# One more pair in seven products, and a new order of the last pairs, in the second run of two down projections

## The chip, the cores and the metric

The kernel runs on one core of a Trainium2 chip. The metric is the device time of one execution in microseconds (us); lower is better. A time of a kernel is the median over several runs. The profile shows one execution more, with every instruction of every engine: PE (TensorE, the matmuls), PEld (its weight loads), DVE (VectorE), ACT (ScalarE), POOL (GpSimd) and SP (SyncE, which here only issues transfers).

## The reference, cut to what matters

The kernel computes one encoder layer on 256 tokens of width 2048: a SwiGLU block, a mixer (gated recurrence and window attention), and a second SwiGLU block, each between RMS norms. The change touches the last matrix product of both SwiGLU blocks, `(silu(gate) * up) @ w_down`:

```python
def swiglu(x, w_gate_up, w_down):
    gate, up = jnp.split(x @ w_gate_up, 2, axis=-1)
    return (jax.nn.silu(gate) * up) @ w_down
...
    for layer in range(DEPTH):
        ff = swiglu(rms_norm(x, pre_norm_ffn1[layer]), w_ffn1_gate_up[layer], w_ffn1_down[layer])
        x = x + 0.5 * rms_norm(ff, post_norm_ffn1[layer])
        ...
        ff = swiglu(rms_norm(x, pre_norm_ffn2[layer]), w_ffn2_gate_up[layer], w_ffn2_down[layer])
        x = x + 0.5 * rms_norm(ff, post_norm_ffn2[layer])
```

`w_down` has 5632 rows and 2048 columns, in float32; the left side is 256 x 5632.

## The kernel before, in words

**Precision.** A float32 product is made of three matmuls in a faster format. Each operand is split into a high part `h` (a rounding copy on ACT, L177) and a low part `l` (source minus high part, on DVE, L178). Then high x high, high x low and low x high are added up in PSUM (`three`, L458 is its matmul).

**Pairs.** The 5632 inner rows are cut into 22 *pairs* of 2 x 128 rows, numbered 0 to 21. The 2048 output columns are cut into two *runs* of 1024. One run takes all 22 pairs and adds them up in four PSUM banks, `c[m][n]` (m: which 128 tokens, n: which 512 columns). So a pair in a run is a 2 x 2 by 2 x 2 block product, and it is done in one of two ways:

- *plain* (`play`, `plain`): eight block products, 24 matmuls of 128 x 128 by 128 x 512;
- *seven* (`products`): Strassen's scheme in Winograd's form, seven block products, 21 matmuls, some of them into four more banks `p`. It needs sums of blocks on both sides. The sums of the left side (`sums[u]`) are made once per pair, on DVE, either when the pair's activations are made (pairs 0 to 14, even) or later by `sums_again` (L1107 to L1114: one instruction of 128 x 512 and four of 128 x 128). Before use they are split in `left_sums` (tile `sp`); for pairs 0 and 2 the split sums of the first run are kept. The sums of the right side come from the weights: two are made by a transfer that adds into the tile (POOL, L1314), two by DVE (L1342, L1343).

At the end of a run a *fold* (`fold`, L548 to L565) combines the `p` banks and adds them into the `c` banks.

**Steps.** The two runs are one list of 44 *steps*, 0 to 43: `orders[0]` and then `orders[1]`; steps 22 to 43 are the second run. All of it is written in order by hand (`manual_schedule`), so each of PE, ACT and DVE works through its instructions as they stand in the code. In step i the loop at L1401 issues:

1. the first part of `splits(i+1)`, the splitting of the next step's weights. For a plain pair that is half 0. For a seven pair it is half 1 (`h`, `l`), the split of the left sums (`sp`), and L1342 and L1343, which need the adding transfer to be done;
2. `prepare(i+4)`, if that step is a seven pair in `added`: its first block is split into the tiles `ha` and `la`, and POOL issues the adding transfer (half a megabyte), behind `la`;
3. transfers that bring back some activations that were put away in DRAM (`fetch`: in the second run pairs 0, 5, 3 and 1, in steps 25, 26, 28 and 29);
4. the second part of `splits(i+1)`: the other half of a plain pair, or the upper sums of a seven pair;
5. the matmuls of step i;
6. for a seven pair, the last part of `splits(i+1)`;
7. `sums_again`, in the steps named in `again_at`.

`ha` and `la` have three buffers each (`rows.firsts = 3`), `h` and `l` five each.

**Weights.** Each step's weights come as one load of a megabyte on SP's queue (L1298) into a tile `raw`. There are five such tiles: three *lasting* ones and two that lie in the pool of the fetched activations (`back`) and may not take the weights of steps 41, 42 and 43 (`coming[0] < NU + 19` in L1294). A load is issued when the splitting of an earlier step has freed a tile (`load_down` at the end of `splits`). The list of loads, `in_order`, is the list of steps with those in `added` moved ahead by 3.5 places. As there are five tiles, a load takes the tile of the step whose splitting ended at that moment, five loads earlier in the list as long as no tile is passed over.

**End of the run.** Pairs 20 and 21 (steps 42 and 43) are *held*: their weights are split in step 40 and after step 41, and their 48 matmuls come bank by bank after the fold has reached each bank (`finish`). Step 41 is the last ordinary one; there the products are sorted by bank, so that the fold can begin. The input `X` of the residual addition (two transfers of a megabyte, L1555) is loaded into the room of the left sums of pairs 0 to 14, after the last of them has been read.

Lines that the prediction names: L177 and L178 (splits), L458 (matmuls), L1107 to L1114 (left sums made later), L1298 (loads), L1314 (adding transfers), L1342 and L1343 (right sums), L1555 (`X`).

Of the kernel before, what the change touches and what calls it, by code (L numbers as in the profile page):

```python
# [37 lines left out]
def hymba_layer_kernel(  # L38
# [37 lines left out]
    def nm(s):  # L76
        uid[0] += 1
        return f"{s}_{uid[0]}"
# [120 lines left out]
    def close_far():  # L199
        far["cm"].__exit__(None, None, None)  # L200
# [719 lines left out]
    def post_pool():  # L920
        return tc.tile_pool(name=nm("post"), bufs=4, reuse_waits="tile")
# [17 lines left out]
    MIXED = range(0, 20, 2)  # L939
# [142 lines left out]
    def ffn(gated, w_dn, post_gain, again, gain=None, lead=None, aside=None):  # L1082

        with ExitStack() as st:
# [6 lines left out]
            hts, sums, away = [], {}, {}  # L1091
# [98 lines left out]
            def some(steps, n):  # L1190
                for _ in range(n):
                    next(steps)
# [21 lines left out]
            def boundary(g, ahead):  # L1214

                a, b = room_for("z"), room_for("s")
                c, (p1, p5, p6, p7) = gated.c, gated.p
                add = nc.vector.tensor_tensor
                rest_of = gated.take(g, last)

                def bank(m, n):
                    for k in range(2):
                        rest_of[4 * k + 2 * m + n]()

                nc.scalar.copy(a, p1)
                add(c[0][0], c[0][0], a, ALU.add)
                add(b, p6, a, ALU.add)
                add(a, p7, b, ALU.add)
                add(c[1][0], c[1][0], a, ALU.add)  # L1229
                bank(0, 0)  # L1230
                bank(1, 0)
                add(b, p5, b, ALU.subtract)
                add(c[0][1], c[0][1], b, ALU.add)
                bank(0, 1)
                add(b, p5, a, ALU.subtract)
                add(c[1][1], c[1][1], b, ALU.add)  # L1236
                bank(1, 1)
                some(ahead, 2)

            def first_pairs(g, waiting):  # L1240

                gated.group(g)
                some(waiting, 1)
                gated.prepare(g, MIXED_IN[1])
                some(waiting, 1)
                ahead = gated.splits(g, 1)
                some(ahead, 2)
                gated.prepare(g, MIXED_IN[2])
                for one in gated.take(g, 0):
                    one()  # L1250
                some(waiting, 1)
                ahead = gated.splits(g, 2)
                some(ahead, 2)
                some(waiting, 1)
                some(ahead, 1)
                for one in gated.take(g, 1):
                    one()

            def pair_ahead(g, u):

                ahead = gated.splits(g, u + 1)
                next(ahead)
                if u + 1 == MIXED_IN[1]:
                    gated.prepare(g, MIXED_IN[3])
                next(ahead)
                for one in gated.take(g, u):
                    one()
                for _ in ahead:
                    pass
                if g == 1 and u == 5:  # L1270
                    sums_in(MIXED_IN[3])
                if u == 5 and 1 < g <= AWAY // 2 + 1:
                    put_away(2 * g - 4)
                    put_away(2 * g - 3)
# [1 line left out]
            orders = [  # L1276
                [9, 11, 8, 13, 10, 15, 12, 1, 0, 3, 14, 5, 16, 17, 2, 7, 4, 19, 6, 18, 20, 21],

                [2, 7, 4, 9, 6, 8, 11, 10, 13, 12, 17, 15, 0, 5, 14, 3, 16, 1, 18, 19, 20, 21],
            ]  # L1280
            added = {0: (12, 0, 14, 16, 2, 4, 6, 18), 1: (*MIXED, 17)}
            steps = [(r, u) for r in range(2) for u in orders[r]]
            in_order = sorted(
                (i - 3.5 if u in added[r] else i, i) for i, (r, u) in enumerate(steps)
# [35 lines left out]
            def splits(i):  # L1320
                if i >= 2 * NU - Pairs.HELD:
                    return
                r, u = steps[i]
                raw = raws[i]
                parts = got[i] = []
                b11, b12, b21, b22 = blocks(raw)
                if not as_seven(r, u):
                    parts.append(split_half(raw, 0))
                    yield
                    parts.append(split_half(raw, 1))  # L1330
                    load_down(raw)
                    yield
                    return
                four = raw.rearrange("p (i c) -> p i c", i=4)
                if i not in firsts:
                    first_block(i)
                    nc.vector.tensor_tensor(
                        four[:, 0:2], four[:, 0::3], four[:, 1:2].to_broadcast([P, 2, 512]), ALU.add
                    )
                parts.append(split_half(raw, 1))  # L1340
                rows.left_sums_ahead(u)
                nc.vector.tensor_tensor(b22, b11, b22, ALU.add)  # L1342
                nc.vector.tensor_tensor(b21, b22, b21, ALU.add)  # L1343
                yield
                parts.append(split_half(raw, 0))
                yield
                parts.append(split_half(raw, 1))
                load_down(raw)
                yield
# [13 lines left out]
            with tc.manual_schedule():  # L1363
                gated.prepare(1, MIXED_IN[0])
                some(gated.splits(1, 0), 2)
                for g in range(1, NG):
                    first_pairs(g, waiting)
                    for u in range(2, last - 1):
                        pair_ahead(g, u)
                    some(gated.splits(g, last), 2)  # L1370
                    if g < NG - 1:
                        gated.prepare(g + 1, MIXED_IN[0])
                    for one in gated.take(g, last - 1):
                        one()
                    boundary(g, gated.splits(g + 1, 0) if g < NG - 1 else splits(0))
                    waiting = units(gated.c, rest)
                    some(waiting, 2)
                room_cm.__exit__(None, None, None)
                close_far()
                back_cm = tc.tile_pool(name=nm("hb"), bufs=AWAY // 2, reuse_waits="tile")  # L1380
                back = back_cm.__enter__()
                fetch_at = {2: (1,), 3: (0,), 5: (3,), 6: (5,), 9: (2,), 10: (7,), 11: (4,), 13: (6,)}
                fetch_at.update({25: (0,), 26: (5,), 28: (3,), 29: (1,)})
                again_at = {8: 16, 14: 18, 24: 17}
                for u in MIXED[8:]:
                    sums[u] = None
                rows = Pairs(w_dn, orders, hts, sums, work, post_gain, near=MIXED[:2])
                rows.firsts = 3
                some(waiting, 2)
                ahead = splits(1)  # L1390
                some(ahead, 2)
                products(0)
                for _ in range(2):
                    load_down(back.tile([P, 2048], F32, tag="raw", name=nm("raw"), bufs=2))
                some(waiting, 1)
                ahead = splits(2)
                some(ahead, 2)
                some(waiting, 1)
                some(ahead, 1)
                products(1)  # L1400
                for i in range(2, 2 * NU - Pairs.HELD):  # L1401
                    if i == NU + 18:
                        back_cm.__exit__(None, None, None)
                        early_cm.__exit__(None, None, None)
                        post = rows.post = st.enter_context(post_pool())
                    ahead = splits(i + 1)
                    next(ahead, None)
                    prepare(i + 4)
                    for u in fetch_at.get(i, ()):
                        fetch(u)  # L1410
                    next(ahead, None)
                    if i == NU + 18:
                        rows.hold(1, raws[2 * NU - 2])
                    products(i)
                    for _ in ahead:
                        pass
                    if i in again_at:
                        sums[again_at[i]] = sums_again(again_at[i])
                    if i == 8:
                        rows.half_gain(far["pool"])  # L1420
                    if i == NU - 1:
                        sums[17] = None
                        rows.second_run()
                        rows.fold_after(NU - Pairs.HELD - 1)
                fold = rows.fold()
                some(fold, 2)
                rows.hold(1, raws[2 * NU - 1])
                for _ in fold:
                    pass
# [951 lines left out]
```

## Time and profile before

| what | before |
|---|---|
| median of 3 runs | 1815.16 us (1814.6 to 1816.67) |
| the profiled execution, its own time | 1816.97 us |
| its span, first to last instruction | 1815.2 us |
| mean granted clock of TensorE | 0.999 |
| DVE busy | 1645.7 us (91%) |
| ACT busy | 1128.2 us (62%) |
| second run of the first down projection | about 590.3 to 703.3 us of the span |
| second run of the second down projection | about 1694.6 to 1807.1 us |

The span is the time between the first and the last instruction in the profile; 1.77 us of the execution lie around it. In the views, a row of a group gives line, engine, operation and tiles, the count, the busy time and the mean duration; a row of the timeline gives start, length, what it is, and in brackets how long the engine was idle before it and what ended the wait. A row of the windows gives, for one stretch, the busy time of each engine with its count, the granted clock, the busy share of the 16 DMA engines and the rate in GB/s.

Where the steps of the end lie, by their matmuls (24 for a plain pair, 21 for a seven pair), first down projection: step 30 begins at 630.57, 31 at 636.01, 32 at 640.77, 33 at 645.53, 34 at 650.97, 35 at 655.73, 36 at 661.17, 37 at 665.93, 38 at 671.37, 39 at 676.13, 40 at 681.57, 41 at 686.33, and the held pairs at 691.77. In the second down projection the steps from 24 on lie 1104.29 us later (step 31 at 1740.30, the held pairs at 1796.06).

### The profile page before, as it was taken

To read this page: it belongs to the slowest core of one execution; us is meant where nothing else is said; L and a number is where in the kernel's file an instruction comes from. 1 tells how busy PE (TensorE), PEld (TensorE's weight loads), DVE (VectorE), ACT (ScalarE), POOL (GpSimd) and SP (SyncE) were. 2 spreads that over 40 slices of the span, in tenths; PEclk is the share of its full clock that TensorE was granted. 3 is DMA by queue.
4 is the path that set the end of the run, shared out by engine and by line. 5 is a ranking of instruction groups with operands and counts; after the bars stand their busy time and mean duration, and the time that the engine had idled before them with its cause. 6 is when DMAs were issued, how large, how long until landed. Compare 5 with 4: busy or idle time off the path is not lost.

```text
span 1815.2 us, 23684 instructions
## 1 busy us (share of the span) xinstructions
PE 1802.6 (99%) x8412; PEld 1496.8 (82%) x8412; DVE 1645.7 (91%) x2149; ACT 1128.2 (62%) x1496; POOL 177.9 (10%) x168
## 2 busy tenths in 40 slices
PE   9999999999999999999999999999999999999998
PEld 7888888888888888888888888888888888888886
DVE  7999999999989988988888888899999999998987
ACT  7565666666565757556676666566666666566663
POOL 1011111111011100110000100111111111011110
PEclk9999999999999999999999999999999999999999
DMA  8889999999699996965655767889999998699994
GB/s 302 240 237 282 276 283 255 254 257 260 212 343 279 280 323 208 296 174 163 174 162 166 245 206 276 244 244 270 284 268 272 255 249 251 192 337 311 263 315 164
DMA packets 217335, 457.06 MB, mean 252 GB/s; under 512 B 13064, under 2 KB 49760, under 8 KB 215936
## 3 DMA queue, kind: packets, MB, share of 16 engines
q1 hardware_dynamic: 181600, 389.07, 61.6%
q0 software_dynamic: 35440, 66.21, 21.4%
q8 instruction: 66, 1.08, 0.2%
q14 instruction: 53, 0.43, 0.1%
q10 hardware_dynamic: 176, 0.27, 0.0%
HBM read 440.80 MB, written 14.70 MB: 251 GB/s over the span
## 4 chain that ended last, share of the span: by engine, by line
PE 88%; DMA 4%; DVE 4%; ACT 2%; issue 1%; SPq 0%; POOL 0%; DVEq 0%; ACTq 0%; POOLq 0%
PE pa L458 40%; PE pb L458 35%; PE pa L326 5%; PE pa L331 3%; DMA raw<-in_w_ffn_gate_up_dram 2%; DVE l L178 2%; DMA raw<-in_w_mix_in_dram 2%; ACT h L177 1%; PE pb L1728 1%; PE pa L1172 1%; PE pb L1172 1%; DMA vr<-in_w_mix_in_dram 1%; PE pa L381 0%; ACT xt L228 0%; PE pa L380 0%
## 5 line engine op out<-in xcount | busy, mean ns | idle before, releaser
L177 ACT CAST h<-raw 128x1024 fp32r<-128x1024 f32 (+1 forms) x846 | 833.0, 1011 | 455.7 <-PE pb L458 152.4
L178 DVE TENSOR_TENSOR l<-raw,h 128x1024 fp32r<-128x1024 f32 (+1 forms) x846 | 963.0, 1170 | 97.6 <-ACT h L177 79.1
L458 PE MATMUL pa<-h,xt 128*128 128x512 f32 x1194 | 418.9, 392 | 0.1
L458 PE MATMUL pb<-h,xt 128*128 128x512 f32 x1038 | 371.0, 392 | 0.4 <-DVE pb L1229 0.4
L458 PEld LDWEIGHTS pa<-h,xt 128*128 128x128 f32 x1194 | 224.2, 188 | 47.9 <-DVE xt L233 0.6
L458 PE MATMUL pa<-l,xt 128*128 128x512 f32 x597 | 233.1, 390 | 0.4 <-DVE l L178 0.4
L458 PEld LDWEIGHTS pb<-h,xt 128*128 128x128 f32 x1038 | 194.8, 188 | 46.5 <-DVE pb L1236 3.7
L458 PE MATMUL pb<-l,xt 128*128 128x512 f32 x519 | 202.3, 390 | 0.0
L1011 POOL DMA_DIRECT2D raw<-in_w_ffn_gate_up_dram x78 | 94.5, 1212 | 733.0 <-DVE l L178 656.9
L458 PE MATMUL pb<-h,ht 128*128 128x512 f32 x452 | 159.2, 389 | 0.0
L458 PE MATMUL pa<-h,ht 128*128 128x512 f32 x452 | 159.2, 389 | 0.0
L458 PEld LDWEIGHTS pa<-l,xt 128*128 128x128 f32 x597 | 112.2, 188 | 23.4 <-DVE l L178 1.7
L458 PE MATMUL pa<-h,xs 128*128 128x512 f32 x332 | 118.6, 389 | 0.0
L458 PE MATMUL pb<-h,xs 128*128 128x512 f32 x332 | 115.7, 389 | 0.0
L458 PEld LDWEIGHTS pb<-l,xt 128*128 128x128 f32 x519 | 97.5, 188 | 18.7
L326 PE MATMUL pa<-xt,h 128*128 128x512 f32 x448 | 109.9, 393 | 0.0
L458 PEld LDWEIGHTS pa<-h,ht 128*128 128x128 f32 x452 | 84.9, 188 | 17.7
L458 PEld LDWEIGHTS pb<-h,ht 128*128 128x128 f32 x452 | 84.8, 188 | 17.7
L326 PEld LDWEIGHTS pa<-xt,h 128*128 128x128 f32 x448 | 81.5, 188 | 15.3
L458 PE MATMUL pa<-l,ht 128*128 128x512 f32 x226 | 87.9, 389 | 0.0
L458 PE MATMUL pb<-l,ht 128*128 128x512 f32 x226 | 87.9, 389 | 0.0
L1314 POOL DMA_DIRECT2D raw<-in_w_ffn_down_dram x38 | 46.1, 1212 | 371.7 <-DVE la L178 320.7
(341 smaller groups left out, 2537.8 us busy)
## 6 DMA issues: line engine op xcount, KB each, us to landing
raw<-in_w_ffn_gate_up_dram SPq DMA_DIRECT2D x350, 512.0 KB, 5.9
raw<-in_w_ffn_down_dram SPq DMA_DIRECT2D x88, 1024.0 KB, 8.1
raw<-in_w_ffn_gate_up_dram POOLq DMA_DIRECT2D x78, 512.0 KB, 8.0
raw<-in_w_mix_in_dram SPq DMA_DIRECT2D x36, 1024.0 KB, 5.1
raw<-in_w_ffn_down_dram POOLq DMA_DIRECT2D x38, 512.0 KB, 10.3
ht<-away SPq DMA_DIRECT2D x24, 512.0 KB, 10.4
raw<-in_w_mix_out_dram SPq DMA_DIRECT2D x12, 1024.0 KB, 6.5
raw<-in_w_mix_in_dram SPq DMA_DIRECT2D x34, 256.0 KB, 5.3
```

The lines of the kernel that those rows point to most:

```text
L177: nc.scalar.copy(hi, src)
L178: nc.vector.tensor_tensor(lo, src, hi.bitcast(F32), ALU.subtract)
L326: nc.tensor.matmul(slot[f], weights(hs, kk, f), xcol(xt, k), start=(k == 0), stop=(k == KT - 1))
L331: nc.tensor.matmul(slot[f][:, 0:T], weights(ls, kk, f), xcol(xt, kh * 8 + kk, 0), start=False, stop=False,)
L458: nc.tensor.matmul(self.bank(at), lhs, rhs, start=(n == 1), stop=n in (ends, self.of[at]), skip_group_check=n > ends,)
L1011: nc.gpsimd.dma_start(raw[:, 0:1024].rearrange("p (k c) -> p k c", k=2), self.source(u, g)[:, :, 1], accum_op=ALU.add,)
L1172: nc.tensor.transpose(bank[:, o : o + P], zs[m][:, k * P : (k + 1) * P], ident)
L1314: nc.gpsimd.dma_start(raws[i][:, 0:1024].rearrange("p (k c) -> p k c", k=2), Pairs.part(w_dn, u, r)[:, :, 512:1024], accum_op=ALU.add,)
L1728: nc.tensor.matmul(dst, left[a], right[b], start=first and i == 0, stop=last and i == 2)
```

## The change

Pair 19 is done in seven products in the second run too, beside pair 17 and the even pairs up to 18. The second run's order from step 35 on is another:

| step | 31 | 32 | 33 | 34 | 35 | 36 | 37 | 38 | 39 | 40 | 41 | 42, 43 |
|---|---|---|---|---|---|---|---|---|---|---|---|---|
| before | 12 s | 17 s | 15 | 0 s | 5 | 14 s | 3 | 16 s | 1 | 18 s | 19 | 20, 21 held |
| after | 12 s | 17 s | 15 | 0 s | 14 s | 5 | 16 s | 19 s | 3 | 18 s | 1 | 20, 21 held |

(s: in seven products.) The left sums of pair 19 are made by `sums_again` in step 30. Its adding transfer is issued like the others, four steps ahead. The code is shared by both down projections.

```diff
             orders = [
                 [9, 11, 8, 13, 10, 15, 12, 1, 0, 3, 14, 5, 16, 17, 2, 7, 4, 19, 6, 18, 20, 21],
 
-                [2, 7, 4, 9, 6, 8, 11, 10, 13, 12, 17, 15, 0, 5, 14, 3, 16, 1, 18, 19, 20, 21],
+                [2, 7, 4, 9, 6, 8, 11, 10, 13, 12, 17, 15, 0, 14, 5, 16, 19, 3, 18, 1, 20, 21],
             ]
-            added = {0: (12, 0, 14, 16, 2, 4, 6, 18), 1: (*MIXED, 17)}
+            added = {0: (12, 0, 14, 16, 2, 4, 6, 18), 1: (*MIXED, 17, 19)}
...
-                again_at = {8: 16, 14: 18, 24: 17}
+                again_at = {8: 16, 14: 18, 24: 17, 30: 19}
...
                     if i == NU - 1:
-                        sums[17] = None
+                        sums[17] = sums[19] = None
                         rows.second_run()
                         rows.fold_after(NU - Pairs.HELD - 1)
```

## The prediction

> **What bounds the kernel now.** First the page: is one engine full? Then the windows of the steps that the change reorders: does that engine ever wait there? Last the chain of waits: what does one step cost?
>
> ```profile
> span 1815.2 us, 23684 instructions
> PE 1802.6 (99%) x8412; PEld 1496.8 (82%) x8412; DVE 1645.7 (91%) x2149; ACT 1128.2 (62%) x1496; POOL 177.9 (10%) x168
> ...
> q1 hardware_dynamic: 181600, 389.07, 61.6%
> q0 software_dynamic: 35440, 66.21, 21.4%
> ...
> PE 88%; DMA 4%; DVE 4%; ACT 2%; issue 1%; SPq 0%; POOL 0%; DVEq 0%; ACTq 0%; POOLq 0%
> ```
>
> PE holds 88% of the chain that ends last. The windows of steps 31 to 40, first and then second down projection (after the times: PE, PEld, DVE, ACT, POOL, clock, DMA share, GB/s):
>
> ```profile
> 640.77:645.53 4.76, 4.76 (x22) 3.94 (x21) 2.27 (x3) 3.35 (x4) 0.04 (x1) 1.00 1.04 367
> ...
> 681.57:686.33 4.76, 4.76 (x22) 3.94 (x21) 3.42 (x4) 4.50 (x6) 0.00 (x0) 1.00 0.19 33
> sum 50.32, PE 50.32 PEld 41.68 DVE 41.66 ACT 31.23 POOL 3.64; mean PE 5.03 PEld 4.17 DVE 4.17 ACT 3.12 POOL 0.36
> ```
> ```profile
> 1785.86:1790.62 4.76, 4.76 (x23) 3.94 (x21) 3.43 (x4) 4.51 (x6) 0.00 (x0) 1.00 0.00 1
> sum 50.32, PE 50.32 PEld 41.67 DVE 41.73 ACT 31.13 POOL 3.64; mean PE 5.03 PEld 4.17 DVE 4.17 ACT 3.11 POOL 0.36
> ```
>
> PE is busy for 50.32 of 50.32 us in both, at full clock. So in this stretch there is no stall to remove: the change can only take matmuls away, or add stalls. The chain in order of time:
>
> ```profile
> 615.78 2.72 PE pa L458 x12
> ...
> 655.90 1.36 PE pa L458 x6
> 657.26 1.36 PE pb L458 x6
> 658.62 1.36 PE pa L458 x6
> 659.98 1.36 PE pb L458 x6
> ...
> 681.74 2.72 PE pa L458 x12
> 684.46 2.04 PE pb L458 x9
> ```
>
> Step 35 (plain) is four rows of 1.36, 5.44 us; step 40 (seven) is 2.72 + 2.04, 4.76 us. One matmul costs 1.36 / 6 = 0.227 us. (These rows lie 0.17 us behind the starts of the matmuls.)
>
> **The change part by part.**
>
> *Three matmuls fewer.* Pair 19 goes from 24 to 21: 5.44 - 4.76 = 0.68 us in each down projection, 1.36 us in all, as long as PE stays full. The Trainium skill's "TensorE: Matmul & The Clock Gate", section "Back-to-back issue gap", gives about 131 ns a matmul of 512 columns in a sustained stream; by that the three would be 0.39 us and the total 0.79. The chain's 0.227 decides.
>
> *DVE's new work.* The timeline of DVE shows one seven pair with its `la`, without an idle time, from one `sp` to the next, and a plain pair further on:
>
> ```profile
> 630.34 0.68 DVE L178 TENSOR_TENSOR sp<-sums,sp 128x512 fp32r<-128x512 f32 x1
> 630.94 0.69 DVE L1342 TENSOR_TENSOR raw<-raw 128x512 f32<-128x512 f32 x1
> 631.66 0.69 DVE L1343 TENSOR_TENSOR raw<-raw 128x512 f32<-128x512 f32 x1
> 632.27 0.69 DVE L178 TENSOR_TENSOR la<-raw,ha 128x512 fp32r<-128x512 f32 x1
> 632.87 3.49 DVE L178 TENSOR_TENSOR l<-raw,h 128x1024 fp32r<-128x1024 f32 x3
> 636.27 0.69 DVE L178 TENSOR_TENSOR sp<-su,sp 128x512 fp32r<-128x512 f32 x1
> ...
> 645.00 2.36 DVE L178 TENSOR_TENSOR l<-raw,h 128x1024 fp32r<-128x1024 f32 x2
> ```
> ```profile
> L1107 DVE TENSOR_TENSOR su<-ht 128x512 f32<-128x512 f32 x1 | 0.7, 685 | 0.0
> L1111 DVE TENSOR_TENSOR su<-su 128x128 f32<-128x128 f32 x1 | 0.3, 293 | 0.0
> ```
>
> A seven pair takes 636.27 - 630.34 = 5.93 us, 0.60 less where no `la` or no `sp` is made beside it; a plain pair 2.36; the late left sums 0.685 + 4 x 0.293 = 1.86. Two sevens and a plain need 14.22 us of DVE beside 14.96 of PE: it keeps up on average. Step by step, x being the time after PE's start of a step at which DVE comes to the split of the next one: step 30 has x = -1.37 (the first row less one split of 1.16, against the start at 630.57); its work is now 5.93 + 1.86, so step 31 has -1.37 + 7.79 - 5.44 = +0.98; step 32 +0.98 + 5.93 - 4.76 = +2.15; step 33 -0.25; step 34 -0.36; step 35 +0.81; step 36 is back at -1.37, where free `h` buffers hold it; 37 -0.88; 38 -0.31; 39 and 40 -1.37. The worst is step 32: half 0 of step 33 is split at 2.15 + 1.16 = 3.31, and PE wants it at 4.76 + 0.23 = 4.99. The old trace stood such a lag without a stall:
>
> ```profile
> 616.73 2.36 DVE L178 TENSOR_TENSOR l<-raw,h 128x1024 fp32r<-128x1024 f32 x2
> ```
>
> Its second split, half 0 of step 28, ends at 619.09, 3.48 us after step 27 began at 615.61. So DVE's extra costs nothing while its lead of 1.68 us lasts; without it each microsecond would be one on PE.
>
> *A new wait.* In steps 31 and 34 `prepare` asks for a fourth `ha` and `la` where three exist, so ACT waits for the first three matmuls of the step, until about 0.9 us into it. Behind it on ACT stand two splits of the next step's weights; DVE comes to `la` only at +0.98 + 3.09 = +4.07 and -0.36 + 3.09 = +2.73. It is hidden: taken at nothing, at most 0.9 us twice in each projection.
>
> *Transfers.* By the queue rows a megabyte costs 0.214 x 1815.2 / 66.21 = 5.87 us of all 16 DMA engines on POOL's queue and 0.616 x 1815.2 / 389.07 = 2.87 on SP's: 3.08 us for an adding transfer of 0.524 MB, 3.01 for a load of 1.049. The windows have a DMA share of 1.04 in step 32 and 0.19 (second time 0.00) in step 40, so the one more adding transfer shifts work into that hole. `X` waits for the `sp` of pair 14, now one step earlier. How late do transfers land? By line, first projection (loads, adding transfers), then the loads of the second:
>
> ```profile
> L1298 SPq DMA_DIRECT2D raw<-in_w_ffn_down_dram x17: 367/368/368, 591.0 to 674.0; - x17
> ...
> DMA to landing us min/median/max: 4.9/7.9/13.0
> ```
> ```profile
> DMA to landing us min/median/max: 7.2/10.1/11.9
> ```
> ```profile
> DMA to landing us min/median/max: 4.9/8.3/14.7
> ```
>
> Adding transfers are issued behind their `la`. Step 35's leaves at 636.01 + 4.7 = 640.7 and, after a median of 10.1, lands at 650.8; L1342 wants it in step 34 at -0.36 + 1.76 = +1.4, 652.4. Steps 37, 38 and 40 come out alike, and PE wants the upper sums some 3 us after that. The tightest load is step 33's, unmoved in the list; it held ACT, then DVE, in the second projection:
>
> ```profile
> 1747.20 1.05 ACT L177 CAST h<-raw 128x1024 fp32r<-128x1024 f32 x1 [3.19 <-DMA raw<-in_w_ffn_down_dram]
> ...
> ```
> ```profile
> 1748.28 1.23 DVE L178 TENSOR_TENSOR l<-raw,h 128x1024 fp32r<-128x1024 f32 x1 [3.02 <-ACT h L177]
> ```
>
> Split at 1749.51, wanted at 1749.82 + 0.23: 0.54 us to spare. It was issued long before the change acts; the new adding transfer leaves at 1745.0, when it is almost in. I keep zero, at most some tenths.
>
> *The last loads come later.* Follow the tiles, each load taking the one freed five loads before. Before, steps 38 and 40 lay in the two `back` tiles; now 36 and 37 do. They may not pass to steps 41 to 43, so these loads wait for the splitting of steps 38, 39 and 40 instead of 36, 37 and 39. SP's timeline before:
>
> ```profile
> 659.96 0.37 SPq L1298 DMA_DIRECT2D raw<-in_w_ffn_down_dram  x1
> 660.38 0.46 SPq L1555 DMA_DIRECT2D X<-in_x_dram  x1
> 664.05 0.37 SPq L1298 DMA_DIRECT2D raw<-in_w_ffn_down_dram  x1
> ```
> ```profile
> 673.96 0.37 SPq L1298 DMA_DIRECT2D raw<-in_w_ffn_down_dram  x1
> ```
>
> These three become: step 41's 4.5 us into step 37 (the -0.88 of above and 5.33), about 670.4; step 42's 0.68 before the old 673.96 (step 39's splitting ends there), 673.3; step 43's 4.0 into step 39 (-1.37 and 5.33), 679.4. The held products begin at 691.77 - 0.68 = 691.1. Step 43's weights are first wanted six matmuls on, at 692.5, and their splitting (1.05 and 1.16) stands before fold additions on DVE: they should land by 689, 9.6 us after the issue. In the hole of the old window a load is near the least of 4.9: it lands around 685. I take zero; the other end is the rival below.
>
> *Sum.* 2 x 0.68 = 1.36 us. Against the profiled execution (span 1815.2, 1816.97 us in all) 1815.6; against the median of the runs, 1.81 lower, 1815.16 - 1.36 = **1813.8 us**, -0.07%.
>
> **The rivals.**
>
> *A, slower: step 43's weights land late.* For it: they leave 5.4 us later than before, and loads here took up to 14.7. Against it: the DMA engines idled then. From 9.6 us on each microsecond of landing is one of PE; at 14.7 it is 5.1 in each projection, 1813.8 + 10.2 = 1824.0. Slower than 0.2% (1818.8) takes 2.5 in each, a landing of 12.1.
>
> *B, the gain is eaten: step 38's weights land late.* Their tile comes free at +0.98 + 5.93 of step 31, 642.9. On ACT `ha` of step 38 stands ahead of the upper sums of step 35, which PE wants at 655.73 + 2.27 = 658.0; less copies and split (0.6 + 1.05 + 1.16), the load must land by 655.2, within 12.3 us. At 13.0 and 14.7 it costs 0.7 and 2.4: 1816.9 us. The median of 7.9 to 8.3 speaks against it; for it, one adding transfer more is in flight beside it. That bears on a rule of the Trainium skill ("DMA: Bandwidth & Descriptors", "Queues, rings and completion order"): each DMA engine takes turns between the queues that have work. By that, a load beside adding transfers gets half the engines' time, 6.0 us for 3.0. The landings agree (4.9 at the least, 13.0 at the most), so B keeps its chance.
>
> *C, pair 19 stays plain*, by a slip in the tables: 1815.2, and 8412 matmuls.
>
> **How the numbers follow.** Forecast 0.72; A 0.12; B 0.12; C 0.02; a gain from something that no row shows 0.02. About 0.2% is what a measurement of this kernel can tell from no change. Faster by more needs 3.6 us and the matmuls give 1.36: 0.02. Slower is A: 0.12. Within: 0.86. The range goes down by the lowest run's distance from the median and a little more (1.4), 1812.4, and up to B and its rounding, 1817.2; A stays outside.
>
> **What would show it.** 8406 matmuls; the window from step 35 to the held products 0.68 us shorter in both projections, PE without idle time; DVE furthest behind in step 32; step 43's load issued near 679.4, landing by 689. The prediction is wrong if PE waits for a low part L178 or `h` before a plain step, or for a fold addition after step 41.

## The result and the profile after

| | before | after |
|---|---|---|
| median of 5 runs each | 1815.5 us (1814.6 to 1816.67) | 1824.43 us (1822.83 to 1825.51) |
| the profiled execution, its own time | 1816.97 us | 1825.32 us |
| first down projection, first to last matmul | 226.79 us | 234.81 us |
| second down projection | 226.31 us | 225.65 us |

The ratio after to before is 1.0047, 95% interval 1.0035 to 1.0058: **0.47% slower**, beyond the 0.2% that a measurement can tell. The forecast was 1813.8 us, the range 1812.4 to 1817.2: the time lies outside the range, and on the other side of the kernel before than was forecast.

The table says already where to look. Both projections run the same code, but for one argument: the first is called with `lead` (L1566), which at its end begins to load and split weights of the next stage, the mixer; the second stands at the end of the program and has none (L2307). The second gained 0.66 us, as forecast (0.68), and the first lost 8.02. The page of after:

```profile
span 1823.5 us, 23709 instructions
PE 1804.1 (99%) x8406; PEld 1498.3 (82%) x8406; DVE 1655.4 (91%) x2169; ACT 1131.5 (62%) x1502; POOL 180.3 (10%) x170
...
q0 software_dynamic: 35984, 67.25, 21.6%
...
L458 PE MATMUL pa<-h,ht 128*128 128x512 f32 x440 | 156.8, 394 | 6.4 <-DVE pa L555 6.4
```

There are 6 matmuls fewer (8406 to 8412), and 1.04 MB more on POOL's queue, two adding transfers: the change does what it says. One row of matmuls has 6.4 us of idle time behind a fold addition (L555). The windows of steps 31 to 40, after, in the first projection and (last row) in the second; the columns are as before:

```profile
682.39:687.15 4.76, 4.76 (x22) 3.94 (x21) 1.23 (x1) 1.05 (x1) 0.00 (x0) 1.00 0.73 253
sum 49.64, PE 49.64 PEld 41.12 DVE 44.33 ACT 29.59 POOL 4.85; mean PE 4.96 PEld 4.11 DVE 4.43 ACT 2.96 POOL 0.49
```
```profile
sum 49.68, PE 49.68 PEld 41.11 DVE 46.47 ACT 32.89 POOL 4.84; mean PE 4.97 PEld 4.11 DVE 4.65 ACT 3.29 POOL 0.48
```

The steps that the change reorders take 49.64 us where they took 50.32, with PE full: no stall among them. The first row is step 40, and it is odd: there ACT was busy for 4.50 us before and is busy for only 1.05 now. Something of its work has gone elsewhere. The waits of PE from the start of the second run to the first held product have one row:

```profile
PE pa L458 <- DVE pa L555: 6.4, 1, 6.4
```

The chain of after through this place, in order of time (start, length, what):

```profile
682.65 1.06 ACT h L177
...
683.73 1.24 DVE l L178
...
684.98 4.95 DMA raw<-in_w_mix_in_dram
...
690.03 1.06 ACT h L177
...
692.26 1.73 DVE l L178 x2
...
694.53 1.22 DVE l L178
695.74 0.61 DVE y L549
...
698.31 0.70 DVE pa L555
...
699.14 6.87 PE pa L458 x20
```

Read it from the bottom: the held products wait for the fold, the fold for low parts on DVE, these for high parts on ACT, and ACT for a *load of the mixer's weights*, the stage behind this projection, which leaves when step 41's split has freed its tile. What does ACT do there? Its timeline and DVE's, after:

```profile
682.65 1.05 ACT L177 CAST h<-raw 128x1024 fp32r<-128x1024 f32 x1 [1.67 <-PE pb L458]
...
690.03 3.89 ACT L177 CAST h<-raw 128x1024 fp32r<-128x1024 f32 x4 [6.33 <-DMA raw<-in_w_mix_in_dram]
691.11 4.63 DVE L178 TENSOR_TENSOR l<-raw,h 128x1024 fp32r<-128x1024 f32 x4 [6.16 <-ACT h L177]
...
693.83 0.58 ACT L548 COPY y<-pa 128x512 f32<-128x512 f32 x1
```

And before:

```profile
681.83 2.95 ACT L177 CAST h<-raw 128x1024 fp32r<-128x1024 f32 x3 [1.68 <-PE pb L458]
...
684.69 0.57 ACT L548 COPY y<-pa 128x512 f32<-128x512 f32 x1
...
689.26 2.00 ACT L177 CAST h<-raw 128x1024 fp32r<-128x1024 f32 x2 [2.11 <-PE pa L458]
```

Before, ACT splits the last half of step 41 and both halves of step 42 in one go (x3), begins the fold (L548), and comes to the mixer's two halves much later (x2 at 689.26). After, it does one half (x1), waits 6.33 us, and then does four: the mixer's two and, *behind* them, step 42's. The fold begins 11.44 us after the start of step 40 (682.39) instead of 3.12 us (681.57), 8.3 us later. The mixer's first split is `lead.load()` (L759) in `finish`. That call stands outside the block that is ordered by hand (`manual_schedule`). The build, which makes one list of instructions for each engine out of the program, has put it ahead of step 42's split in after and behind step 43's in before.

Then the clock. Four-microsecond windows from 690, after:

```profile
690.00:694.00 4.00, 2.76 (x13) 1.94 (x11) 2.89 (x3) 3.97 (x5) 0.00 (x0) 1.00 0.14 58
694.00:698.00 4.00, 0.00 (x0) 0.00 (x0) 3.93 (x6) 2.29 (x3) 0.00 (x0) 0.84 0.83 269
698.00:702.00 4.00, 2.85 (x7) 2.31 (x8) 4.00 (x6) 0.00 (x0) 0.00 (x0) 0.50 0.67 255
702.00:706.00 4.00, 4.00 (x16) 3.21 (x15) 1.85 (x4) 1.62 (x3) 0.00 (x0) 0.80 0.78 262
706.00:710.00 4.00, 4.00 (x20) 3.30 (x19) 2.75 (x5) 2.83 (x5) 0.56 (x1) 1.00 0.00 0
...
699.14:706.76 7.62, 7.62 (x24) 6.10 (x25) 5.47 (x7) 1.62 (x3) 0.00 (x0) 0.71 0.61 210
```

PE stands still in the second row and the granted clock falls to 0.50 in the third. The first 24 held products take 7.62 us; at 0.227 each they would take 5.45. So the slower products behind the pause cost 2.17 us more. The sum: from the last matmul of step 41 to the first held product 6.78 us instead of 0.23, 6.55 lost; the slower products, 2.18 over all 48; three matmuls fewer, -0.68: 8.05 of the measured 8.02.

### The profile page after: what moved, and what is told of

The parts are those of the page before. It is cut to its first block, busy times and chain, and to the rows that moved or that the text cites. A ratio compares the mean times of both kernels' runs of the same rounds, so it can differ in the third digit from the quotient of the medians.

```text
span 1823.5 us, 23709 instructions
## 1 busy us (share of the span) xinstructions
PE 1804.1 (99%) x8406; PEld 1498.3 (82%) x8406; DVE 1655.4 (91%) x2169; ACT 1131.5 (62%) x1502; POOL 180.3 (10%) x170
## 4 chain that ended last, share of the span: by engine, by line
PE 91%; DVE 4%; DMA 3%; ACT 1%; issue 1%; SPq 0%; DVEq 0%; POOL 0%; ACTq 0%; POOLq 0%
PE pa L458 41%; PE pb L458 36%; PE pa L326 5%; PE pa L331 3%; DVE l L178 2%; DMA raw<-in_w_mix_in_dram 2%; PE pa L381 1%; PE pa L380 1%; DMA raw<-in_w_ffn_gate_up_dram 1%; PE pa L379 1%; PE pb L1728 1%; ACT h L177 1%; PE pa L1172 1%; PE pb L1172 1%; PE pb L2029 0%
## 5 line engine op out<-in xcount | busy, mean ns | idle before, releaser
L458 PE MATMUL pb<-h,ht 128*128 128x512 f32 x440 | 155.2, 389 | 0.0
```

What stands on the lines that cost most here:

```text
L458: nc.tensor.matmul(self.bank(at), lhs, rhs, start=(n == 1), stop=n in (ends, self.of[at]), skip_group_check=n > ends,)
```

## The experiments

**The theory.** The loss is the place of the mixer's first split on ACT and DVE, and nothing else; without it the change gains what was forecast. **Rivals:** the seventh product of pair 19 (DVE, transfers), the new turn of the pairs, or the later loads.

**1. The split tied behind step 43's.** In the kernel after:

```diff
-        nc.scalar.copy(hi, src)
+        last["split"] = nc.scalar.copy(hi, src)
...
-            if lead:
+            if lead and mul == 0.5:
+                with tc.issue_after(last["split"].ins):
+                    lead.load()
+            elif lead:
                 lead.load()
```

> The changed kernel, with one tie more: the split of the next stage's first weights (the mixer's, which the end of the first down projection loads ahead) may not stand on ACT before the last split of the held pairs. Loads, tiles, order of the pairs and seven products of pair 19 stay as changed. Theory H (ACT and, behind it, DVE stand behind that split, which waits for a load that is issued only when step 41's splitting frees its tile): the stall of 6.55 us before the held products of the first projection goes, and the slow matmuls after it (2.18 us) too, so 0.68 us less than before in each projection: about 1814.1 us, 0.9993 of before. Theory L (the loads of steps 41 to 43, which come later since their tiles are freed later, hold the end back): nothing changes, 1824. Theory D (one more seven pair overloads DVE or the DMA engines, and the end pays): nothing changes, 1824.

Measured: 1815.05 us (1813.87 to 1816.46; before beside it 1815.79), ratio 0.9996, interval 0.9987 to 1.0005. ACT's timeline has the old shape again:

```profile
682.61 2.95 ACT L177 CAST h<-raw 128x1024 fp32r<-128x1024 f32 x3 [1.67 <-PE pb L458]
...
690.23 2.00 ACT L177 CAST h<-raw 128x1024 fp32r<-128x1024 f32 x2 [2.16 <-DMA raw<-in_w_mix_in_dram]
```

The pause is gone, and some 9 us with it (8.0 in the first projection: 226.83 us instead of 234.81), with pair 19 still in seven products and the pairs in the new turn. The second projection takes 225.64 us. The first one's gain is missing, for the most part because of a short pause at step 33:

```profile
644.69 2.94 ACT L177 CAST h<-raw 128x1024 fp32r<-128x1024 f32 x3 [2.20 <-DMA raw<-in_w_ffn_down_dram]
...
647.05 0.50 PE L458 MATMUL pa<-l,ht 128*128 128x512 f32 x1 [0.38 <-DVE l L178]
```

Step 33's weights land late, and PE loses 0.54 us (0.77 from matmul to matmul, where 0.23 is usual).

**2. The split moved ahead by hand, in the kernel before.** The other direction: nothing of the change, only the call, ahead of step 42's split.

```diff
                     if i == NU + 18:
+                        if lead:
+                            lead.load()
                         rows.hold(1, raws[2 * NU - 2])
...
-            if lead:
+            if lead and mul != 0.5:
                 lead.load()
```

> The kernel before, with one edit: in the first down projection the loads and the split of the mixer's first weights are written ahead of the split of pair 20 (step 42), in step 40. Order of the pairs, seven products and the loads of steps 41 to 43 stay as before. Theory H: the whole loss without the change: the load leaves at about 684.0 (when step 41's splitting frees a tile), lands about 5 us later, and PE goes on 9.1 us after that (as in the changed kernel: 690.03 to 699.14), at 698.1 instead of 691.8; with the slow matmuls after it, 6.4 + 2.2 = 8.6 us: about 1824.1 us, 1.0047 of before. Theories L and D: the change is not in it, so 1815.5.

Measured: 1824.82 us (1824.09 to 1825.77; before 1815.79), ratio 1.0050, interval 1.0037 to 1.0064. ACT and PE of this run:

```profile
688.09 3.89 ACT L177 CAST h<-raw 128x1024 fp32r<-128x1024 f32 x4 [6.45 <-PE pa L458]
...
697.21 0.76 PE L458 MATMUL pa<-h,ht 128*128 128x512 f32 x1 [6.50 <-DVE pa L555]
```

The same four in a row after the same wait (the releaser named is another here, since a wait goes down to whatever came last; the mixer's load landed at 687.99), and the same pause. The place of that one split makes the whole loss, in either kernel.

**3. What moves it? The order without the seventh product.** The kernel after with pair 19 plain again: 19 taken out of `added[1]`, of `again_at` and of the line that clears its sums.

> The changed kernel with pair 19 plain again (no late left sums, no adding transfer for it): only the order of the last pairs is new. In the built program the split of the mixer's first weights stands ahead of step 42's on ACT, as in the changed kernel. Theory H: the same stall, and no matmuls saved: 1815.5 + 8.6 = about 1824.1 us, 1.0047; in the trace ACT's long wait is for the mixer's weights. Theory L: also slow, but ACT's long wait is for step 42's or 43's weights. Theory D: 1815.5, since the added work is gone.

Measured: 1825.01 us (1824.49 to 1826.5; before 1815.79), ratio 1.0053, interval 1.0039 to 1.0066. ACT again:

```profile
687.86 3.89 ACT L177 CAST h<-raw 128x1024 fp32r<-128x1024 f32 x4 [6.51 <-DMA raw<-in_w_mix_in_dram]
```

So the order alone brings the loss; the seventh product isn't needed for it.

**4. Two pairs exchanged, and nothing else.** The kernel before, pair 19 plain; only

```diff
-                [2, 7, 4, 9, 6, 8, 11, 10, 13, 12, 17, 15, 0, 5, 14, 3, 16, 1, 18, 19, 20, 21],
+                [2, 7, 4, 9, 6, 8, 11, 10, 13, 12, 17, 15, 0, 5, 14, 3, 16, 19, 18, 1, 20, 21],
```

> The kernel before, pair 19 plain as there, with pairs 1 and 19 exchanged in the second run's order and nothing else, so that pair 1 is worked on in step 41. Theory: this exchange alone moves the next stage's first split ahead of step 42's, ScalarE waits about 6 us for its load, TensorE pauses 6 to 7 us before the held products and runs at half its rate for some 24 products after; 1823 to 1826 us, most likely 1824.5. Rival (the loss needs the new turn of pairs or the seventh product): 1814.5 to 1816.5 us.

Measured: 1825.24 us (1823.87 to 1826.48; before 1815.54), ratio 1.0046, interval 1.0032 to 1.0060.

```profile
689.97 3.89 ACT L177 CAST h<-raw 128x1024 fp32r<-128x1024 f32 x4 [6.42 <-PE pa L458]
```

The mixer's load landed at 689.87 here. Pair 1 in step 41 is enough. It has the same number of matmuls in the same kinds of steps as pair 19 there.

**5. Another pair last.** The kernel after, all of the change and no tie, with the tail 5, 0, 14, 3, 16, 19, 1, 18, 15: two sevens and a plain one in turn as in after, but pair 15 in step 41.

> The changed kernel, pair 19 in seven products and all, with only the order of the second run's tail different: its last eight pairs before the held ones are 5, 0, 14, 3, 16, 19, 1, 18 and then 15, so that step 41 works on pair 15, whose activations lie in the main pool, and pair 1, whose activations lie in the pool of fetched tiles, is done by step 39. Nothing ties the next stage's first split. Theory (the next stage's split is put ahead of step 42's wherever the last tile of the fetched pool is used as late as step 41): ScalarE splits step 42 right behind step 41, TensorE has no pause before the held products, the time is 1813.5 to 1815.5 us, most likely 1814.4. Rival (seven products for pair 19, or two seven-product pairs and a plain one in turn, cost the time by themselves): 1823 to 1825, with the 6 us pause in front of the held products.

Measured: 1814.33 us (1813.51 to 1815.33; before 1815.54), ratio 0.9988, interval 0.9979 to 0.9997: 0.12% faster than the kernel before. That is less than the 0.2% named above, but the interval leaves 1 out. ACT, and PE's only wait in the two second runs (it is in the second projection, at step 33):

```profile
679.76 2.95 ACT L177 CAST h<-raw 128x1024 fp32r<-128x1024 f32 x3 [1.68 <-PE pb L458]
...
689.03 2.00 ACT L177 CAST h<-raw 128x1024 fp32r<-128x1024 f32 x2 [3.81 <-DMA raw<-in_w_mix_in_dram]
```
```profile
PE pa L458 <- DVE l L178: 0.8, 1, 0.8
```

**6. What about pair 1?** Its activations lie in a pool that step 40 closes; so far the theory said, the pool of the fetched ones. But step 40 closes two:

```python
                    if i == NU + 18:
                        back_cm.__exit__(None, None, None)
                        early_cm.__exit__(None, None, None)
                        post = rows.post = st.enter_context(post_pool())
```

`back` holds the fetched pairs, `early` pairs 8 to 13; the pool of pairs 14 to 21 stays open. The run with pair 15 last, but with pair 13 (never fetched, in `early`) in step 41:

```diff
-                [2, 7, 4, 9, 6, 8, 11, 10, 13, 12, 17, 15, 0, 14, 5, 16, 19, 3, 18, 1, 20, 21],
+                [2, 7, 4, 9, 6, 8, 11, 10, 5, 12, 17, 15, 0, 14, 3, 16, 19, 1, 18, 13, 20, 21],
```

> The run with pair 15 in step 41, but with pair 13 in step 41 in its place (the tail is 11, 10, 5, 12, 17, 15, 0, 14, 3, 16, 19, 1, 18, 13). Pair 13's activations were never put away and fetched again; they lie in the second pool that step 40 closes, the one of pairs 8 to 13, while those of pair 15 lie in the pool of pairs 14 to 21, which stays open. Theory as put for the earlier runs (it takes a pair of the fetched pool): no early split of the next stage, 1813.5 to 1816. Theory, widened (any pair of a pool that step 40 closes, read in step 41): ScalarE has the next stage's first split ahead of step 42's, waits some 6 us, TensorE pauses 6 to 7 us and runs at about half rate for some 2 us worth of lost time after; 1823 to 1826 us.

Measured: 1823.66 us (1822.71 to 1825.51; before 1816.15), ratio 1.0041, interval 1.0026 to 1.0055.

```profile
689.31 3.89 ACT L177 CAST h<-raw 128x1024 fp32r<-128x1024 f32 x4 [6.53 <-DMA raw<-in_w_mix_in_dram]
```

The narrow form of the theory fell. The wide one fits all kernels without a tie (the one of run 7 too, where the loads differ):

| step 41 works on | its pool | mixer's split | time, us |
|---|---|---|---|
| pair 19 (before) | stays open | behind step 43's | 1815.5 |
| pair 15 (runs 5 and 10) | stays open | behind step 43's | 1814.33; 1814.0 |
| pair 1 (after; order only; exchange only) | `back`, closed in step 40 | ahead of step 42's | 1824.43; 1825.01; 1825.24 |
| pair 13 | `early`, closed in step 40 | ahead of step 42's | 1823.66 |

The held pairs' `h` and `l` go into `post`, which is opened over the room of the closed pools. That the build, when it lays the order, takes step 42's split to wait for that room until step 41 has read its pair, and fills the hole on ACT with the next stage's split, is an inference from this table, not shown: how the build decides leaves no row in a trace. On the chip step 42's split had no need to wait for step 41's products: in run 1 ACT splits step 42 right behind step 41, from 682.61 on, while step 41's matmuls begin at 687.12.

**7. How much hangs on the mixer's load?** The kernel after, with step 41's weights (and theirs alone) allowed into a `back` tile, so that the mixer's tile comes free earlier.

```diff
-                if coming and (coming[0] < NU + 19 or any(raw is one for one in gated.lasting)):
+                if coming and (coming[0] < NU + 20 or any(raw is one for one in gated.lasting)):
```

> The changed kernel with the bound for the two tiles in the back pool one step higher, so that step 41's weights may lie there: the loads of steps 41, 42 and 43 then leave when steps 36, 38 and 39 are split, as early as before or nearly, and the mixer's first load takes the tile of step 40, free some 4.4 us earlier than step 41's. The split of the mixer's weights still stands ahead of step 42's. Theory H: the wait for the mixer's load shrinks by those 4.4 us: it leaves at about 679.6, lands at 684.6, PE could go on at 693.7 and would have at 691.1, so a stall of about 2.6 us is left in the first projection: about 1816.7 us, up to 1818 if the matmuls after it are slow as well. Theory L: with the early loads back the whole stall goes: 1814.1. Theory D: 1824.

Measured: 1819.1 us (1817.09 to 1823.96; before 1815.79), ratio 1.0020, interval 1.0011 to 1.0029. The time is some 1 us above what was expected; the profiled execution, 1817.09, is within it. SP and ACT, then the windows of the pause and behind it:

```profile
678.24 8.95 SPq L153 DMA_DIRECT2D raw<-in_w_mix_in_dram  x2
...
683.34 3.90 ACT L177 CAST h<-raw 128x1024 fp32r<-128x1024 f32 x4 [2.59 <-DMA raw<-in_w_mix_in_dram]
...
692.46 0.47 PE L458 MATMUL pa<-h,ht 128*128 128x512 f32 x1 [2.64 <-DVE pa L555]
```
```profile
689.43:692.46 3.03, 0.39 (x3) 0.04 (x1) 2.96 (x6) 0.19 (x1) 0.00 (x0) 1.00 1.00 380
692.46:696.46 4.00, 4.00 (x17) 3.19 (x18) 4.00 (x6) 0.95 (x3) 0.00 (x0) 1.00 0.89 306
```

The order is the wrong one still, but the load leaves at 678.24 instead of 684.98. ACT waits 2.59 us and PE 2.64; after it was 6.33 and 6.39. The pause is as long as the wait for the load. If that holds down to no wait at all, the two foreign splits in themselves (some 2 us on ACT) are paid by the fold's old slack: before, L555 ended at 689.66, 2.1 us before the held products. After this short pause the clock stayed at 1.00. The wide spread of this kernel's runs (up to 1823.96) would fit a clock that drops in some of them: the seven runs with a mean clock of 0.997 or 0.998 are all slower than the three at 0.999. That is argued, not shown, since only one of them has a trace.

**8. The old order, with pair 19 in seven products.** Is the new turn of pairs needed? The kernel before with pairs 1 and 19 exchanged, 19 in seven products as in after, and the tie of run 1; steps 38, 39 and 40 are then three sevens in a row.

> Pair 19 in seven products, but the order of the kernel before with pairs 1 and 19 changed about (0 s, 5, 14 s, 3, 16 s, 19 s, 18 s, 1: three seven pairs in a row at the end), and with the tie of e1 that keeps the mixer's split behind the held pairs. By the sums of the prediction (DVE 5.33 us for each of these seven pairs beside 4.76 of PE, with a lead of 1.4 us and more) three in a row cost PE nothing: 1.36 us saved, about 1814.3, the same as e1; the new order would then not be needed for the gain. If DVE can't hold three in a row, PE waits in steps 39 to 41: 1.7 us and more lost, 1816 and up.

Measured: 1820.16 us (1819.23 to 1821.81; before 1816.46), ratio 1.0021, interval 1.0012 to 1.0030: a miss by 6 us. Step 37's weights come late, and DVE can't make it up beside three sevens (their load on SP's queue, then ACT and DVE):

```profile
652.71 0.37 SPq L1301 DMA_DIRECT2D raw<-in_w_ffn_down_dram  x1
...
662.70 1.05 ACT L177 CAST h<-raw 128x1024 fp32r<-128x1024 f32 x1 [5.55 <-DMA raw<-in_w_ffn_down_dram]
...
663.78 1.23 DVE L178 TENSOR_TENSOR l<-raw,h 128x1024 fp32r<-128x1024 f32 x1 [4.92 <-ACT h L177]
```
The load leaves 177.8 us after the projection's first matmul and takes 9.9 us; before, step 37's left after 174.8 us and took 6.7. The list of loads shows why it leaves later: pair 19 in step 39 is now a seven pair, and its load is moved ahead of step 37's. From 663.78 to the first addition of the fold into a bank (L555), which ends at 691.02, DVE has no idle time. In it the three seven pairs in a row begin 5.49 us apart (their `sp` at 667.80, 673.29 and 678.78) beside 4.76 us of PE. PE loses time at steps 37 and 42 in both projections and at 33 in the second; they take 228.12 and 229.45 us. So the seventh product pays in the new turn and not in the old. The expectation had neither the moved load nor the fold behind a late DVE.

**9 and 10. The pause at step 33.** Runs 1 and 5 lost 0.5 and 1.2 us there, in one projection each. Runs 6 (0.6) and 8 (0.8) lost time there too, and so did runs 2 (0.2 and 0.6) and 4 (0.5), where pair 19 is plain and the order up to step 38 is the old one. So the pause doesn't come from the change; it isn't in every execution, and the two profiled ones of before and after have none. SP's timeline of run 1 (in it three lines more stand ahead, so L1298 and L1139 are L1301 and L1142):

```profile
627.96 0.46 SPq L1142 DMA_DIRECT2D ht<-away  x1
630.08 6.66 SPq L1301 DMA_DIRECT2D raw<-in_w_ffn_down_dram  x2
```

The load of step 33's weights is the first of the two in the second row. It leaves right behind a fetch and lands 14.5 us later. Two kernels fetch the activations of pairs 3 and 1 later: run 1 with

```diff
-                fetch_at.update({25: (0,), 26: (5,), 28: (3,), 29: (1,)})
+                fetch_at.update({25: (0,), 26: (5,), 36: (3,), 38: (1,)})
```

> The kernel of e1_split_behind with one edit: the activations of pairs 3 and 1 are fetched in steps 36 and 38 instead of 28 and 29 (they are used in steps 39 and 41). In the trace of e1 one matmul of step 33 waited 0.54 us in the first projection, for weights that were loaded 13 us before beside those two fetches. If the fetches are what makes that load late, it lands some 3 us earlier (1 MB less ahead of it, at 2.87 us a megabyte), the 0.54 us goes, and the time is 0.0 to 0.6 us under e1's, 1814.1 to 1814.7 beside a kernel before at 1815.5 to 1815.8. If the adding transfers make it late, step 33's load lands as late as before and the time is e1's. If the fetched activations now come late, steps 39 or 41 wait and it is slower than e1.

and run 5 with `33: (3,), 36: (1,)`:

> The run with pair 15 in step 41, and the activations of pairs 3 and 1 fetched in steps 33 and 36 and not in 28 and 29. If the 0.5 us pause in step 33 comes from weights held up behind those two fetches, it is gone and the time is 0.3 to 0.9 us under that of the run without the later fetches, 1813.2 to 1814.4 us. Rival (the pause comes from elsewhere, or the later fetches hold up the loads of steps 36 to 39): no difference, or up to 2 us slower.

Measured: 1813.88 us (1813.24 to 1815.38; before 1816.46), ratio 0.9987, interval 0.9978 to 0.9996; and 1814.0 us (1813.41 to 1815.28; before 1815.54), ratio 0.9988, interval 0.9979 to 0.9997. PE waits nowhere in the second runs of either; the projections take 226.12 and 225.65 us in both, 0.67 and 0.66 under the kernel before. The loads issued from 620 to 640, in run 1 and in the first of these:

```profile
DMA to landing us min/median/max: 9.7/10.7/14.5
```
```profile
DMA to landing us min/median/max: 8.3/9.3/9.6
```

The pause is gone, and the loads land earlier. The ten profiled kernels with the old fetches have 20 projections between them. In these the load of step 33's weights takes 13.0 to 15.4 us, and PE loses time at step 33 in just the seven where it takes 14.5 us or more (14.3 at most in the other 13). With the later fetches it takes 8.4 to 9.9 us in all four. Against runs 1 and 5 the medians differ by 1.17 us (beside a slower set of the kernel before) and by 0.33 us: that the kernel as a whole is faster for it isn't settled. Both beat the kernel before by about 0.12%, as run 5 does: with 11 runs to 21 the intervals leave 1 out. The kernel before with the later fetches was not run, so what they would do for it isn't known.

## Why the prediction was wrong, point by point

**The step that failed** is "The held products begin at 691.77 - 0.68 = 691.1", with the order of ACT and DVE behind step 41 taken from the old trace. Less the 1.5 us by which this execution began its first projection later (478.0 against 476.5), they began at 697.6. The prediction followed each load and each split of the hand-written list, and the list did what it says; but `finish` stands outside the list, and the first work in it on ACT and DVE is the split of another stage's weights. Where that one goes was settled by the build, and not alike for the two kernels; the prediction took its place for fixed. Experiments 1 and 2 show that this place is the whole loss, in both directions; 4, 5 and 6 show that the pair in step 41 decides it.

*Three matmuls fewer*, 0.68 each: right. 0.66 in the second projection, 0.67 in both where nothing else interferes (runs 9 and 10). The 131 ns a matmul of the Trainium skill (the section named in the prediction) would have given 0.39.

*DVE's new work*: right. It was to come to step 33's split 2.15 us into step 32, at 644.42 in this trace; it ends the split ahead of it at 642.21 + 2.35 = 644.56 and then waits for ACT:

```profile
642.21 2.35 DVE L178 TENSOR_TENSOR l<-raw,h 128x1024 fp32r<-128x1024 f32 x2
...
644.97 3.50 DVE L178 TENSOR_TENSOR l<-raw,h 128x1024 fp32r<-128x1024 f32 x3 [0.40 <-ACT h L177]
```

*The new wait for `ha`* is there, until 638.39, 0.88 us into step 31 (forecast 0.9), and nothing waits for it on PE:

```profile
638.39 0.62 ACT L177 CAST ha<-raw 128x512 fp32r<-128x512 f32 x1 [1.77 <-PE pa L458]
```

*Transfers*: right in after itself, where the adding transfers of the first projection's second run land after a median of 9.4 us (10.1 before). "Zero, at most some tenths" at step 33 was too little: other runs lost 0.5 to 1.2 us there, with the change and without it.

*The last loads*: right. Steps 41, 42 and 43 (from 672.5 to 681.2, or 670.9 to 679.7 without the later start; forecast 670.4, 673.3, 679.4), and they land in 4.9 to 6.4 us:

```profile
L1298 SPq DMA_DIRECT2D raw<-in_w_ffn_down_dram x3: 368/368/368, 672.5 to 681.2; - x3
...
DMA to landing us min/median/max: 4.9/5.0/6.4
```

*Rival A* came out at the same 1824 us, and at the same place, the fold addition ahead of the held products; that is chance, and it was still wrong. Its mechanism was step 43's weights landing late; they landed at 686.1, 684.6 without the later start, where 685 was forecast. Its price of 5.1 us in each projection isn't what was paid: 8.0 in one and nothing in the other. *Rival B* didn't happen: step 38's weights left at 644.59 and took 7.3 us. None of the rivals asked what *else* ACT and DVE could be given at that place; the prediction's last sentence, PE waiting "for a fold addition after step 41", named the sign without a mechanism for it. Even there the price would have been too low, as none of its terms has the clock: 2.2 of the 8.7 us lost.

## What to carry to other kernels

When an edit changes which tiles are alive at a boundary, an instruction that stands outside the hand-ordered part can be placed among those that were laid by hand: compare, engine by engine, the order of the built kernel before and after, most of all near the places where pools are closed and opened. Here one early split held up all that stood behind it on ACT, and PE paused for as long as ACT waited for that split's data (6.39 and 6.33 us). Tie such an instruction behind the last one that must go first, or keep the old order of lifetimes, and price a pause of PE with the slower products that follow it.

## What the runs showed of the hardware

The granted clock of TensorE falls in a long pause and comes back only some time after it. After the pause of 6.4 us in after it stood at 0.50 for a while (window 698 to 702), and the next 24 products took 7.62 us instead of 5.45. If it is either full or half, the shares of the three windows (0.84, 0.50, 0.80) make it half for 1.3 + 4.0 + 1.6 = 6.9 us, from 4 us after the last matmul to 4.4 us after the first new one. After a pause of 2.6 us (run 7) it stayed at 1.00. The Trainium skill's "TensorE: Matmul & The Clock Gate", section "HAM oscillation — how this bites in real kernels", puts the limit at gaps of about 3.4 us; these two pauses lie on either side of it and agree.

The pauses of runs 2, 3, 4 and 6 are alike (6.5 to 6.6 us), but the clock falls at 2.6, 2.3, 3.7 and 5.1 us after the last matmul, and it is at half for 6.8, 10.2, 6.8 and 6.8 us. So the first 24 held products took 6.94, 8.37, 7.48 and 8.04 us: nearly equal pauses cost 1.5 to 2.9 us behind them. In run 3 the clock fell earlier in the pause than run 7's pause was long; whether a pause of 2.6 us always leaves the clock alone is therefore open.
